# A decoder layer on one core: two pools at the seam of its phases, and GpSimd's mixer work on VectorE

## The chip, the cores and the metric

The kernel runs on one core of a Trainium2 chip. The metric is the time of one execution on the device in microseconds. The kernel before took 2881.92 us in the median of three runs (2880.78 to 2887.45).

## The reference

One post-norm decoder layer in float32 for 2048 tokens of width 1024. The input is modulated and projected by one weight matrix into a gated short convolution (512 channels) and an RWKV-7 time mixing (8 heads of 64); both go through one output projection, a normalisation, a SwiGLU feed-forward part of width 2816 and a second normalisation.

```python
h = x * (1.0 + sc1) + sh1
p = h @ w_in[l]
y_conv = short_conv_mixer(p[..., :N_CONV_COLS], conv_w[l])
y_rwkv = rwkv7_mixer(p[..., N_CONV_COLS:], ...)   # p + mu * (token_shift(p) - p), then a delta-rule scan
mix = jnp.concatenate([y_conv, y_rwkv], axis=-1) @ w_out[l]
x = layer_norm(DEEPNORM_ALPHA * x + (1.0 + gt1) * mix, ln1_g[l], ln1_b[l])
h = x * (1.0 + sc2) + sh2
gate, up = jnp.split(h @ w_ffn_in[l], 2, axis=-1)
f = (jax.nn.silu(gate) * up) @ w_ffn_out[l]
x = layer_norm(DEEPNORM_ALPHA * x + (1.0 + gt2) * f, ln2_g[l], ln2_b[l])
```

## The kernel before, in words

**Products.** Each float32 operand is split into a high half (`act.copy`, a rounding on ScalarE) and a lower half (raw minus high), and a product takes three matmuls (`split`, L230 to L233; `mm3`, L235). The high half is always ScalarE's; the lower half goes to GpSimd (`pool`) unless the caller names VectorE (`dve`).

**Phase 1** (the `with` block at L371) goes over four quarters of 512 tokens. For each quarter `dense` (L259) streams the input weights in half tiles: `half_weight` (L250) loads 256 KB into `raw` (3 buffers), and splits them into `wh` and `wl` (4 buffers each), its lower half on GpSimd. `shifted` (L424) evicts a projected tile with the token shift: ScalarE scales it, VectorE adds the shifted columns, and ScalarE copies the last column into `carry` for the next quarter (L433). Each quarter has four units of two heads (`unit`, L438): preparation (three of its products, `BK` L494, `rk` L497 and `R` L513, are GpSimd's), masked chunk matrices, a triangular solve on VectorE with a small layout through DRAM (`Np` to `Nd` to `Ns`, and back from `Gd` to `H16`, L585 to L609), four further small matmul steps, the chunk scan with one eviction `S` per chunk (L698), and a tail that normalises and stores to `yT` (L734). The solve's first matmul `pz` (L620) reads `LT`, which VectorE transposes from the layout that returns (L613).

**Order of TensorE's work.** TensorE's order is written out by a planner, `Interleave` (L72): the dense stream runs, and units and normalisations are side tasks that yield a cost and a time until their next step. `D_GH` (L51, 15.0) is that time between the issue of the layout that returns and `LT`. The other engines' orders come from the framework's scheduler. All loads and stores are issued by SP, in order.

**The seam.** The output projection of the third quarter runs while the last unit ends. Phase 2 (`with` at L1034) opens the pool `fa` in the memory that phase 1's pool `rw` leaves; a tile of `fa` waits only for the tiles of `rw` whose memory it takes. The tiles named `at...` (L397, L1037) fix the order in memory. `moving(0)` (L1046) makes the first half's moving operands for the feed-forward product: a Strassen-like scheme with seven products (`PRODS`, L976), each with four k of 128. For each k it loads four blocks of h2d (L1057; three into `rawx`, 4 buffers, one into `xr`, 2 buffers), and makes all seven operands of that k: five are a sum on VectorE first (`bh` or `us`, L988), then a high half `uh` on ScalarE and a lower half `ul`, alternately on VectorE and GpSimd. TensorE then takes the products one after the other, each over all four k (L1124 to L1134), 84 matmuls for one block of 128 hidden columns.

**Later.** `weights` (L1091) makes seven weight operands for each block, sums on VectorE, high halves on ScalarE, lower halves `wl` on GpSimd. In the second half of the tokens `scale_weights` (L1165) goes along with the products from the fifth block on: it loads 44 pieces of w_ffn_out, multiplies them on GpSimd with the gate row (L1172), and stores them to `wfs`, for the last product. The last product makes all lower halves (`fl`, `ol`) on VectorE (L1258, L1273).

Of the kernel before, what the change touches and what calls it, by code (L numbers as in the profile page):

```python
# [11 lines left out]
F32 = mybir.dt.float32  # L12
# [7 lines left out]
P = 128  # L20
# [30 lines left out]
D_ST, D_NS, D_TR, D_GH = 1.1, 13.0, 2.0, 15.0  # L51
# [20 lines left out]
class Interleave:  # L72
# [31 lines left out]
    def __call__(self, stream, last=True):  # L104

        more = True
        while more or any(last or not t[3] for t in self.tasks):
            if self.side():
                continue
            cost = next(stream, 0) if more else None  # L110
            if cost == 0:
                more = False
            elif cost is not None:
                self.now += cost
            elif self.tasks and not self.side():
                self.now = min(t for t in [t[0] for t in self.tasks] + self.banks if t > self.now)


@with_exitstack
def kernel(  # L120
# [129 lines left out]
    def half_weight(src, name):  # L250

        raw = f512("raw", "r" + name, 3)
        load(out=raw, in_=src)
        wh = f512("wh", "h" + name, 4, F32R)
        wl = f512("wl", "l" + name, 4, F32R)
        split(wh, wl, raw)
        return wh, wl
# [113 lines left out]
    with ExitStack() as ph1:  # L371
        rw = ph1.enter_context(tc.tile_pool(name="rw", bufs=1))
# [23 lines left out]

        for tag, bufs in (("yc", 1), ("yo", 1), ("sg", 2)):  # L397
            rw.tile([P, QT], F32, tag=tag, name="at" + tag, bufs=bufs)

# [24 lines left out]
        def shifted(q, ps, i, o):  # L424

            a = t2k("A", "A", 1)
            act.activation(a, ps, AF.Identity, scale=omu[:, i:i + 1])
            m = mu[:, i:i + 1]
            dve.scalar_tensor_tensor(out=o[:, 1:QT], in0=ps[:, 0:QT - 1], scalar=m, in1=a[:, 1:QT],
                                     op0=ALU.mult, op1=ALU.add)  # L430
            dve.scalar_tensor_tensor(out=o[:, 0:1], in0=carry[:, q % 2, i:i + 1], scalar=m, in1=a[:, 0:1],
                                     op0=ALU.mult, op1=ALU.add)
            act.copy(out=carry[:, 1 - q % 2, i:i + 1], in_=ps[:, QT - 1:QT])  # L433

        def c3(ap):
            return ap.rearrange("p (c t) -> p c t", t=C)

        def unit(n, q, hp, r, kx, vx, lo):  # L438
# [55 lines left out]
            pool.tensor_tensor(out=BK[:, :, C:2 * C], in0=c3(kP), in1=c3(x2), op=ALU.mult)  # L494

            rk = t2k("sq", "rk" + u)
            pool.tensor_tensor(out=rk, in0=kx, in1=mk, op=ALU.mult)  # L497
# [15 lines left out]
            pool.tensor_tensor(out=R, in0=c3(r), in1=Pc[:, :, 1:C + 1], op=ALU.mult)  # L513
# [520 lines left out]
    with ExitStack() as ph2:  # L1034
        fa = ph2.enter_context(tc.tile_pool(name="fa", bufs=1, reuse_waits="tile"))

        for tag, bufs in (("h26", 8), ("h22", 8), ("h27", 8), ("h24", 8), ("h21", 8), ("h25", 8), ("rawx", 4),  # L1037
                          ("h23", 8), ("us", 1)):
            fa.tile([P, 512], F32, tag=tag, name="at" + tag, bufs=bufs)
# [6 lines left out]
        def moving(half):  # L1046
# [18 lines left out]
            if half == 0:  # L1065
                sums = cycle(lambda: hb[:, 0, :], lambda: hb[:, 1, :], own)
                for k in range(4):
                    raws = {}
                    for b in names:
                        t = (lnp.tile([P, 512], F32, tag="xr", name=f"b{k}_{b}", bufs=2) if b == "21" else  # L1070
                             fa.tile([P, 512], F32, tag="rawx", name=f"b{k}_{b}", bufs=4))
                        raws[b] = fetch(t, b, k)
                    for n, (i, _, terms) in enumerate(PRODS):
                        operand(i, k, terms, raws, n + k)
# [90 lines left out]
        def scale_weights():  # L1165

            for ff in range(FT):
                for m in range(2):
# [3 lines left out]
                    pool.tensor_tensor(out=w, in0=w, in1=rw3[0][:, ms], op=ALU.mult)  # L1172
# [242 lines left out]
```

## Time and profile before

| what | value |
|---|---|
| median of three runs | 2881.92 us (2880.78 to 2887.45) |
| the profiled execution, its own time | 2881.27 us |
| its span, first to last instruction | 2879.5 us |
| TensorE busy (matmuls) | 2660.8 us, 92% |
| VectorE busy | 1898.7 us, 66% |
| ScalarE busy | 1098.7 us, 38% |
| GpSimd busy | 1148.7 us, 40% |
| mean granted clock of TensorE | 0.955 |

In the rows below PE is TensorE's matmuls, PEld its weight loads, DVE VectorE, ACT ScalarE, POOL GpSimd, and SPq the queue of SP, which issues the loads and stores. A name such as `L233` is a line of the kernel, and that line may be a helper's, so the tiles (`uh<-b`: written, then read) say which use it is. A row of waits says who stood still, what released it, for how many microseconds in total, how often, and the longest.

### The profile page before, as it was taken

The numbers are of one execution on the slowest core, as the hardware profiler recorded it, in microseconds if no ns is written. First come the engines' busy times: TensorE is split into PE (matmuls) and PEld (weight loads), VectorE is DVE, ScalarE is ACT, GpSimd is POOL, SyncE is SP. The second block draws the span as 40 slices with busy tenths as digits, with TensorE's granted clock in tenths as the row PEclk, the third lists the DMA queues.
The fourth block names the chain that finished last, engine by engine and source line by source line (L and its number), as shares of the span: only waits on it lengthen the run. The fifth ranks groups of instructions, "written<-read, shape, count | busy, mean of one in ns | idle before, by whom it ended". The sixth has DMA issues, their size and how long they took to land.

```text
span 2879.5 us, 50206 instructions
## 1 busy us (share of the span) xinstructions
PE 2660.8 (92%) x19232; PEld 2082.8 (72%) x19232; DVE 1898.7 (66%) x3133; ACT 1098.7 (38%) x1995; POOL 1148.7 (40%) x935
## 2 busy tenths in 40 slices
PE   7788999999999899998599999997999999998998
PEld 5566677776777677766477788875767887887786
DVE  7354655556445655554573777788988778659697
ACT  4554433334432433434353533333223333332352
POOL 4665333323333333332453544457886442000011
PEclk8888999989999999999799999998999999999999
DMA  6443322233322222224253533233664336655673
GB/s 236 139 129 116 91 62 70 73 104 119 120 69 69 84 66 69 77 72 156 92 179 128 169 105 106 99 99 121 219 213 138 107 102 222 207 179 186 202 237 106
DMA packets 248344, 369.86 MB, mean 128 GB/s; under 512 B 58660, under 2 KB 81188, under 8 KB 248104
## 3 DMA queue, kind: packets, MB, share of 16 engines
q1 hardware_dynamic: 248104, 366.65, 39.5%
q8 instruction: 151, 2.47, 0.3%
q14 instruction: 89, 0.73, 0.1%
HBM read 278.99 MB, written 87.56 MB: 127 GB/s over the span
## 4 chain that ended last, share of the span: by engine, by line
PE 40%; DVE 5%; DMA 4%; POOL 2%; issue 1%; ACT 0%; SPq 0%; POOLq 0%; DVEq 0%; ACTq 0%
PE f L238 8%; PE f L237 8%; PE f L236 8%; PE o L237 4%; PE o L238 4%; PE o L236 4%; PE do L270 3%; DMA wf<-in_wfo_dram 2%; DMA wfs<-wf 2%; POOL wf L1172 1%; DVE c L1007 1%; DVE ws L988 1%; DMA b<-h2d 0%; DVE ul L233 0%; POOL wl L233 0%
## 5 line engine op out<-in xcount | busy, mean ns | idle before, releaser
L236 PE MATMUL f<-uh,wh 128*128 128x512 f32 x1232 | 495.8, 402 | 32.2 <-ACT uh L232 27.7
L238 PE MATMUL f<-uh,wl 128*128 128x512 f32 x1232 | 495.1, 402 | 19.9 <-POOL wl L233 19.7
L237 PE MATMUL f<-ul,wh 128*128 128x512 f32 x1232 | 494.0, 401 | 12.0 <-DVE ul L233 7.2
L233 POOL TENSOR_TENSOR l<-r,h 128x512 fp32r<-128x512 f32 x201 | 265.2, 1321 | 444.8 <-ACT h L232 359.5
L233 POOL TENSOR_TENSOR wl<-ws,wh 128x512 fp32r<-128x512 f32 x220 | 316.3, 1439 | 296.7 <-ACT wh L232 259.5
L236 PEld LDWEIGHTS f<-uh,wh 128*128 128x128 f32 x1232 | 234.8, 191 | 92.8 <-ACT uh L232 31.8
L238 PEld LDWEIGHTS f<-uh,wl 128*128 128x128 f32 x1232 | 234.8, 191 | 85.6 <-POOL wl L233 30.5
L237 PEld LDWEIGHTS f<-ul,wh 128*128 128x128 f32 x1232 | 234.8, 191 | 72.2 <-DVE ul L233 9.4
L232 ACT CAST wh<-ws 128x512 fp32r<-128x512 f32 x220 | 136.7, 621 | 364.7 <-DVE ws L988 259.0
L1007 DVE TENSOR_TENSOR c<-f,c 128x512 f32<-128x512 f32 x264 | 181.2, 687 | 127.6 <-PE f L238 69.7
L988 DVE TENSOR_TENSOR ws<-w,w 128x512 f32<-128x512 f32 x275 | 242.8, 907 | 18.0 <-DMA w<-wfs 7.4
L237 PE MATMUL o<-ol,fh 128*128 128x512 f32 x616 | 243.3, 395 | 8.9 <-DVE ol L233 8.9
L236 PE MATMUL o<-oh,fh 128*128 128x512 f32 x616 | 242.1, 393 | 4.2 <-DVE c L1007 4.1
L238 PE MATMUL o<-oh,fl 128*128 128x512 f32 x616 | 243.7, 396 | 0.0
L232 ACT CAST h<-r 128x512 fp32r<-128x512 f32 x201 | 123.5, 616 | 215.6 <-PE d L270 157.5
L232 ACT CAST fh<-fr 128x512 fp32r<-128x512 f32 x154 | 95.7, 621 | 237.4 <-PE o L237 160.5
L291 POOL TENSOR_SCALAR rsb<-mvb 128x1 f32<-128x1 f32 x16 | 5.7, 356 | 430.2 <-DVE mvb L289 419.6
L233 DVE TENSOR_TENSOR fl<-fr,fh 128x512 fp32r<-128x512 f32 x154 | 106.2, 693 | 94.1 <-ACT fh L232 85.8
L233 POOL TENSOR_TENSOR lo<-ro,ho 128x512 fp32r<-128x512 f32 x64 | 83.6, 1312 | 198.3 <-ACT ho L232 148.4
L233 POOL TENSOR_TENSOR wl<-w,wh 128x512 fp32r<-128x512 f32 x88 | 127.4, 1448 | 49.4 <-ACT wh L232 49.4
L237 PEld LDWEIGHTS o<-ol,fh 128*128 128x128 f32 x616 | 116.7, 189 | 37.1 <-DVE ol L233 10.6
L236 PEld LDWEIGHTS o<-oh,fh 128*128 128x128 f32 x616 | 116.7, 189 | 31.3 <-DVE c L1007 5.7
(498 smaller groups left out, 5800.1 us busy)
## 6 DMA issues: line engine op xcount, KB each, us to landing
r<-in_win_dram SPq DMA_DIRECT2D x201, 256.0 KB
w<-in_wfi_dram SPq DMA_DIRECT2D x176, 256.0 KB
fr<-fd SPq DMA_DIRECT2D x154, 256.0 KB
w<-wfs SPq DMA_DIRECT2D x132, 256.0 KB
fd<-fs SPq DMA_DIRECT2D x110, 256.0 KB
wm<-in_wmod_dram SPq DMA_DIRECT2D x72, 256.0 KB
ro<-in_wout_dram SPq DMA_DIRECT2D x64, 256.0 KB
fd<-th SPq DMA_DIRECT2D x44, 256.0 KB
```

The costliest lines, as they stand in the source:

```text
L232: act.copy(out=hi, in_=raw)
L233: (lo_eng or pool).tensor_sub(lo, raw, hi)
L236: pe.matmul(ps, lh, rh, start=start, stop=False)
L237: pe.matmul(ps, lh, rl, start=False, stop=False)
L238: pe.matmul(ps, ll, rh, start=False, stop=stop)
L270: pe.matmul(ps, l[:, ks], r, start=kk == 0 and i == 0, stop=kk == KT - 1 and i == 2)
L291: pool.tensor_scalar(rs[:, 0:1], mv[:, 1:2], LN_EPS, None, ALU.add)
L988: (eng or dve).tensor_tensor(out=out, in0=blocks[a], in1=blocks[b.lstrip("-")], op=ALU.subtract if b[0] == "-" else ALU.add)
L1007: dve.tensor_tensor(out=c[b, t], in0=in0, in1=in1, op=op)
L1172: pool.tensor_tensor(out=w, in0=w, in1=rw3[0][:, ms], op=ALU.mult)
```

## The change

Seven edits, in the order of the diff: `D_GH` is 18 instead of 15. A class `Pools` sends each tile of a phase to one of two pools by its tag, one from the left and one from the right of the memory; in phase 1 the tags of `EARLY1` go to the left, in phase 2 those of `EARLY2`, so that the tiles of `EARLY2` lie over those of `EARLY1`, and the tiles that fixed the order go. `half_weight` makes its lower half on VectorE. The carry of the token shift is VectorE's. The three products of a unit are VectorE's. `moving(0)` makes the operands of two products for all four k, then of two more, then of three, and loads for each group and k the blocks that it needs, 36 loads instead of 16. `scale_weights` multiplies on VectorE.

```diff
-D_ST, D_NS, D_TR, D_GH = 1.1, 13.0, 2.0, 15.0
+D_ST, D_NS, D_TR, D_GH = 1.1, 13.0, 2.0, 18.0
...
+class Pools:
+    def __init__(self, first, second, early):
+        self.pools, self.early = (second, first), early
+    def tile(self, shape, dtype, name, tag=None, bufs=1):
+        return self.pools[(tag or name) in self.early].tile(shape, dtype, tag=tag or name, name=name, bufs=bufs)
+
+EARLY1 = ("uph", "upl", "blkr", "Ak", "BK", "x2", "tz", "Pi", "ta", "nb", "sq", "cg", "r", "A", "th", "tl", "k", "v", "z", "AK")
+EARLY2 = ("rawx", "h23", "h25", "us")
...
-        split(wh, wl, raw)
+        split(wh, wl, raw, dve)
...
-        rw = ph1.enter_context(tc.tile_pool(name="rw", bufs=1))
+        rw = Pools(ph1.enter_context(tc.tile_pool(name="rw", bufs=1)),
+                   ph1.enter_context(tc.tile_pool(name="rwb", bufs=1, side="right")), EARLY1)
...
-        for tag, bufs in (("yc", 1), ("yo", 1), ("sg", 2)):
-            rw.tile([P, QT], F32, tag=tag, name="at" + tag, bufs=bufs)
...
-            act.copy(out=carry[:, 1 - q % 2, i:i + 1], in_=ps[:, QT - 1:QT])
+            dve.tensor_copy(carry[:, 1 - q % 2, i:i + 1], ps[:, QT - 1:QT])
...
-            pool.tensor_tensor(out=BK[:, :, C:2 * C], in0=c3(kP), in1=c3(x2), op=ALU.mult)
+            dve.tensor_tensor(out=BK[:, :, C:2 * C], in0=c3(kP), in1=c3(x2), op=ALU.mult)
...
-            pool.tensor_tensor(out=rk, in0=kx, in1=mk, op=ALU.mult)
+            dve.tensor_tensor(out=rk, in0=kx, in1=mk, op=ALU.mult)
...
-            pool.tensor_tensor(out=R, in0=c3(r), in1=Pc[:, :, 1:C + 1], op=ALU.mult)
+            dve.tensor_tensor(out=R, in0=c3(r), in1=Pc[:, :, 1:C + 1], op=ALU.mult)
...
-        fa = ph2.enter_context(tc.tile_pool(name="fa", bufs=1, reuse_waits="tile"))
-        for tag, bufs in (("h26", 8), ("h22", 8), ("h27", 8), ("h24", 8), ("h21", 8), ("h25", 8), ("rawx", 4),
-                          ("h23", 8), ("us", 1)):
-            fa.tile([P, 512], F32, tag=tag, name="at" + tag, bufs=bufs)
+        fa = Pools(ph2.enter_context(tc.tile_pool(name="fa", bufs=1, reuse_waits="tile")),
+                   ph2.enter_context(tc.tile_pool(name="fab", bufs=1, reuse_waits="tile", side="right")), EARLY2)
...
-                for k in range(4):
-                    raws = {}
-                    for b in names:
-                        t = (lnp.tile([P, 512], F32, tag="xr", name=f"b{k}_{b}", bufs=2) if b == "21" else
-                             fa.tile([P, 512], F32, tag="rawx", name=f"b{k}_{b}", bufs=4))
-                        raws[b] = fetch(t, b, k)
-                    for n, (i, _, terms) in enumerate(PRODS):
-                        operand(i, k, terms, raws, n + k)
+                for prods in (PRODS[:2], PRODS[2:4], PRODS[4:]):
+                    for k in range(4):
+                        raws = {}
+                        for b in names:
+                            if any(b in (x.lstrip("-") for x in terms) for _, _, terms in prods):
+                                t = (lnp.tile([P, 512], F32, tag="xr", name=f"b{k}_{b}", bufs=2) if b == "21" else
+                                     fa.tile([P, 512], F32, tag="rawx", name=f"b{k}_{b}", bufs=4))
+                                raws[b] = fetch(t, b, k)
+                        for n, (i, _, terms) in enumerate(prods):
+                            operand(i, k, terms, raws, n + k)
...
-                    pool.tensor_tensor(out=w, in0=w, in1=rw3[0][:, ms], op=ALU.mult)
+                    dve.tensor_tensor(out=w, in0=w, in1=rw3[0][:, ms], op=ALU.mult)
```

## Rows read from the trace of the kernel before

**Rows 1.** Stretches: start:end, length, busy of PE, PEld, DVE, ACT, POOL; clock, DMA, GB/s

```profile
130.00:1300.00 1170.00, 1092.92 (x12032) 835.54 (x12030) 641.51 (x1331) 462.43 (x876) 447.38 (x394) 0.96 0.29 88
1300.00:1402.00 102.00, 91.56 (x783) 71.15 (x782) 46.66 (x95) 43.87 (x86) 30.88 (x33) 0.93 0.42 131
1402.00:1452.00 50.00, 15.35 (x34) 9.28 (x35) 38.02 (x44) 19.77 (x33) 27.02 (x19) 0.56 0.33 106
1452.00:1466.00 14.00, 14.00 (x66) 11.38 (x65) 11.00 (x20) 10.98 (x19) 9.46 (x12) 1.00 0.62 225
2000.00:2200.00 200.00, 184.73 (x763) 142.44 (x762) 180.19 (x181) 57.95 (x100) 171.54 (x108) 0.99 0.61 204
2200.00:2400.00 200.00, 200.00 (x859) 161.15 (x858) 153.42 (x200) 65.97 (x113) 96.14 (x73) 1.00 0.30 102
```

**Rows 2.** Waits of PE from 1402 to 1452, grouped by instruction

```profile
L236 PE MATMUL f<-uh,wh 128*128 128x512 f32 x9 | 6.3, 702 | 26.0 <-ACT uh L232 26.0
```

**Rows 3.** Timeline of SP's queue at the seam: start, length, instruction

```profile
1362.16 0.36 SPq L352 DMA_DIRECT2D h2d<-hb  x1
...
1401.75 0.33 SPq L734 DMA_DIRECT2D yT<-yg  x1
1402.12 32.45 SPq L1057 DMA_DIRECT2D b<-h2d  x14
```

**Rows 4.** Groups of VectorE's instructions, 1402 to 1452: count, busy, mean ns, idle before

```profile
L988 DVE TENSOR_TENSOR bh<-b,b 128x512 f32<-128x512 f32 x14 | 13.1, 955 | 8.2 <-DMA b<-h2d 8.2
...
L233 DVE TENSOR_TENSOR ul<-bh,uh 128x512 fp32r<-128x512 f32 x7 | 7.1, 1033 | 0.8 <-ACT uh L232 0.7
```

**Rows 5.** One stretch at the start of the seam, columns as in rows 1

```profile
1402.00:1407.50 5.50, 0.00 (x0) 0.00 (x0) 0.63 (x2) 0.63 (x2) 0.00 (x0) 0.68 0.73 237
```

**Rows 6.** Groups of instructions, 130 to 1300: two of GpSimd, one of VectorE

```profile
L233 POOL TENSOR_TENSOR l<-r,h 128x512 fp32r<-128x512 f32 x186 | 245.9, 1324 | 443.8 <-ACT h L232 358.6 <-PE d L270 34.1 <-PE s L697 17.6
...
L497 POOL TENSOR_TENSOR rk<-k,ta 128x512 f32<-128x512 f32 x15 | 22.3, 1490 | 29.0 <-ACT ta L476 24.7 <-PE ss L484 4.2
...
L572 DVE TENSOR_TENSOR Ym<-sr,kst 128x512 f32<-128x512 f32 x30 | 19.3, 685 | 28.9 <-PE sr L568 28.9
```

**Rows 7.** Who TensorE waited for in the whole span: total us, times, longest us

```profile
PE pz L620 <- DVE LT L613: 18.5, 7, 5.9
...
PE s L697 <- DVE S L698: 8.3, 4, 3.6
PE d L270 <- DVE h_5l L774: 8.0, 2, 5.3
...
PE b L523 <- ACT rkh L232: 5.5, 2, 3.3
```

**Rows 8.** Timeline of ScalarE and VectorE around one carry in the first quarter

```profile
79.31 0.14 ACT L433 COPY carry<-d 128x1 f32<-128x1 f32 x1
...
78.92 0.21 DVE L431 SCALAR_TENSOR_TENSOR k<-carry,vecs,A 128x1 f32<-128x1 f32 x1
```

**Rows 9.** Waits of TensorE from 2000 to 2200

```profile
PE f L238 <- POOL wl L233: 15.1, 17, 1.8
```

**Rows 10.** Groups of instructions of GpSimd and VectorE, 2000 to 2200

```profile
L1172 POOL TENSOR_TENSOR wf<-wf,rws 128x512 f32<-128x512 f32 x43 | 65.3, 1523 | 19.8 <-DMA wf<-in_wfo_dram 12.6 <-issue 5.5 <-POOL wl L233 1.4
...
L988 DVE TENSOR_TENSOR ws<-w,w 128x512 f32<-128x512 f32 x46 | 63.1, 1396 | 4.8 <-DMA w<-in_wfi_dram 4.2 <-issue 0.6
...
L988 DVE TENSOR_TENSOR fs<-th,th 128x512 f32<-128x512 f32 x25 | 32.4, 1342 | 0.7
```

**Rows 11.** The sums of VectorE from 2200 to 2400

```profile
L988 DVE TENSOR_TENSOR ws<-w,w 128x512 f32<-128x512 f32 x53 | 41.0, 808 | 0.0
```

**Rows 12.** Waits of GpSimd from 130 to 1300

```profile
POOL l L233 <- ACT h L232: 358.6, 110, 10.9
```

**Rows 13.** Two waits of the whole span that belong to the last product

```profile
DVE fl L233 <- ACT fh L232: 85.8, 59, 2.3
...
PE o L237 <- DVE ol L233: 8.9, 4, 6.1
```

## The prediction

> **What bounds the kernel now.** I read the stretches first, then who kept TensorE waiting in each, then the queues behind those waits. TensorE is the bound nearly everywhere: in the main part of phase 1 it is busy 1093 of 1170 us, and in a steady stretch of phase 2 it is busy 200 of 200 us with 859 matmuls, 0.233 us each [rows 1]. So a change pays only where TensorE stands still. The reader is to see three such places. The largest is the seam between the phases: in the 50 us from 1402 TensorE is busy 15.4 us, and the granted clock is 0.56, that is, mostly its 1.2 GHz level after standing still, while VectorE is busy 38 us [rows 1]. The second is 2000 to 2200, where TensorE loses 15.3 us with GpSimd busy 171.5 us [rows 1]. The third is spread over phase 1, in single waits of 1 to 6 us.
>
> At the seam the waits are for the first operands of the feed-forward part: 26.0 us for the high half `uh` [rows 2]. What they wait for stood in SP's queue: fourteen loads of h2d issue only from 1402.1, and take 32.5 us to issue, though the last store of the h2d that they read was issued at 1362.2 [rows 3]. Forty microseconds went by with the data there. The code says why: the tiles of `fa` lie in the memory of `rw`, whose last unit stores its output at 1401.8 [rows 3], and the loop makes all seven products' operands of k=0 before it turns to k=1, so that the first product, which needs its four k, waits for 22 of the 28 operands.
>
> **The change part by part.**
>
> *Seam (two pools, three groups of products).* What the first two products need (`rawx`, h23, h25, `us`: 21 tiles) now lies over tiles of `rw` that are dead when the last unit's middle is made, so their eight loads and eight operands can be made between 1362 and 1402, where VectorE is busy under half of the time (46.7 of 102 us from 1300) [rows 1]. They cost VectorE four sums of 0.96 us and four lower halves of at most 1.03 us [rows 4], about 8 us; GpSimd makes the other four. Behind 1402 stand 20 operands. VectorE's work there is its 38.0 us [rows 1] less these 8: 30 us, so 1432 at the earliest. The loads grow from 16 to 36 (2, 3 and 4 for each k, by the code). Eight are early, and six more fit into the free `rawx` and `xr`; 22 remain. After 1402 five moves of 262 KB (the store and four loads) took 5.5 us at 237 GB/s [rows 5], 1.1 us each, so 22 take 24 us, 1426, and the buffers keep the two from overlapping fully. I take 1434 for the last operand, and 1440 for the end of the first block of seven products, since two products (24 matmuls of 0.233 us) stand behind it. Before, 26 of the 84 matmuls were done by 1452 (34, less eight that are transposes by the code), the other 58 take 13.5 us and stand, with eight transposes, in the 14 us to 1466 [rows 1], where the block ends. Gain **26 us**. Bounds: if TensorE never waits, 84 matmuls and two transposes end at 1422, gain 44; if each of the eight later steps of k loads first and then computes, 8 x (3.9 + 3.8) = 61 us to 1463, and 5.6 us more, gain -3. I choose by the VectorE row, because loads of one k and sums of the one before can run together while there are spare buffers.
>
> The Trainium skill, "DMA: Bandwidth & Descriptors", section on bandwidth, speaks against reloading in pieces: it wants transfers of 1 MiB and lists 0.95 us for 64 KB and 6.15 us for 1 MB. Between these a 256 KB load would be some 1.9 us (an estimate from that page), 22 of them 42 us, and the gain 16 us rather than 26. The row of five moves at 1.1 us each decides here, so I keep 26.
>
> *Phase 1, work moved from GpSimd to VectorE.* The lower halves of the streamed weights, 186 in the main part of the phase at 1.32 us on GpSimd [rows 6], 64 more in the output projections, and three mixer products in each of 16 units, such as `rk` at 1.49 us [rows 6]. On VectorE such an operation takes 0.685 us where nothing disturbs it, as the mask of the scan does [rows 6]. That is about 300 x 0.69 = 207 us more on VectorE over some 1500 us, from 55% busy [rows 1] to about 65%, since something comes back: beside GpSimd's work VectorE's own two-operand instructions are stretched, such as a sum to 1.396 us where GpSimd is busiest, against 0.808 in a calmer stretch [rows 10, 11]. None of GpSimd's moved work kept TensorE waiting in phase 1 except through `rk`: the wait for `rkh` is 5.5 us [rows 7]. Taking that product and its queue away gains **4 us** (0 to 5.5). What is late next is VectorE itself: weights have four buffers, about 11 us of cover, so a lower half that comes late is hidden, but the scan's evictions now queue behind lower halves. TensorE's largest waits for VectorE there, other than the layout, are S with 8.3 us and the operands at the start of a quarter, h, with 8.0 [rows 7], and a dozen smaller kinds; I let the busier queue lengthen these two by half: cost **8 us** (bounds: 5 us gained by the shorter instructions, and the second rival).
>
> *Carry on VectorE.* TensorE waits for the carry a few times at the start of the phase, but the carry is only last by a hair: where it ended a wait at 79.45, VectorE's own reading of the same bank had ended at 79.13 [rows 8]. The copy there takes about as long as the 0.21 us of the one-column instruction ahead of it. **0 us** (-2 to 3); ScalarE loses 56 short copies and some idling that nothing waits for.
>
> *Later time for the layout (D_GH 15 to 18).* TensorE waits 18.5 us in seven waits for LT [rows 7]. Three microseconds later, and filled with dense work, takes up to 3 us from each: of the largest, 5.9 us [rows 7], 2.9 stay. At most 15 us; I take **11**, since the last unit has little left to fill with. A unit's chain ends 3 us later, which at the end of the phase can cost 3 us once: lower bound -3.
>
> *Scaling of w_ffn_out on VectorE.* From 2000 to 2200 TensorE waits 15.1 us for GpSimd's `wl` in 17 waits [rows 9]; 43 scalings take 65.3 us of GpSimd there [rows 10]. Without them GpSimd has 106 us of 200, about the 96 of the next stretch [rows 1], where TensorE loses nothing. VectorE, at 180 us of 200, gets 43 x 0.69 to 0.81 = 30 to 35 us, and gets back the stretching: 46 sums at 1.396 against 0.808 us in the next stretch, 27 us, and 25 sums `fs` at 1.34 against 0.69, 16 us [rows 10, 11]. So about 170 of 188 us, tight but under the bound. What it must now wait for are the scaling's loads, 12.6 us of GpSimd's idling now [rows 10], in line ahead of sums and evictions. Gain **11 us** (bounds: 15; and -5, if all of those waits fall on a full VectorE).
>
> **Sum.** 26 + 4 - 8 + 0 + 11 + 11 = 44 us. The profiled execution took 2881.27 us (span 2879.5), 0.65 us under the median of 2881.92, so the sum goes against either: 2838 us.
>
> **The rivals.**
>
> *A. The seam closes by half.* The operands' memory isn't free as early as the code suggests, or SP holds the h2d loads behind weight loads that wait for a buffer, so the first group starts at 1402 after all. Then only the order by groups helps: 36 loads of 1.1 us end at 1442, the last operand stands at about 1448, the block ends at 1454, gain 12 rather than 26: 2852 us. For it: SP's queue is in order, and the loads stood behind the last unit's store at 1401.8. Against it: that store needn't stand ahead of them once the memory is free.
>
> *B. VectorE's queue holds the scan: slower.* In phase 1 GpSimd's lower halves waited 358.6 us for ScalarE's high halves, 110 times, 3.26 us each [rows 12]; on GpSimd this held nobody. On VectorE, in order, whatever stands behind such a wait stands still, S and Np evictions among them. If one in five of the 110 holds an eviction that TensorE needs, 22 x 3.26 = 72 us come in the place of the 8 us counted: 2901 us. It decides from 16 such waits on, one in seven, where the 52 us that the rest gains are used up. Against it: in the last phase VectorE makes the lower halves `fl` in just this way, waits 85.8 us in 59 waits for ScalarE, and TensorE loses 8.9 us to it [rows 13]. The Trainium skill, "TensorE: Matmul & The Clock Gate", in its table at the head, calls VectorE's queue strictly first in, first out, which is what this rival needs; the row on `fl` agrees with it and shows it cheap where no scan stands behind it.
>
> *C. The seam closes wholly*, sums of the second group being made early as well: 44 us there instead of 26, 2820 us. Against it: the tiles of the next products (h21 first) lie over `gu`, which the last unit reads at 1400.
>
> *D. Gains of A with a dearer queue*: seam 12, the queue 28 instead of 8: 2872 us and up, about no change.
>
> **How the numbers follow.** Forecast 0.63, A 0.16, C 0.07, D 0.06, B 0.08. A measurement of this kernel can tell about 0.3%, 9 us, from no change. Faster by more: forecast, A, C and a little of D, 0.87; within it 0.05, slower 0.08. The range takes in C with the layout's and the scaling's upper bounds (2803), and on the other side A and D's near end with the scaling's lower bound (2873).
>
> **What would show it.** In the changed profile: h2d loads issued from about 1365 and again well before the end of the first phase; TensorE busy about half of the 50 us behind the seam, or more, and few waits for `uh` before the first 24 matmuls; waits for LT down to 4 to 7 us; no wait for `wl` near 2000 to 2200 above 4 us, with VectorE under 95%; TensorE's waits for VectorE in phase 1 no more than 10 us above the present. It is wrong if the h2d loads still start behind the last unit's store (A), if waits for S and the h operands grow by tens of microseconds (B), or if the block behind the seam ends within 25 us of its start (C).

## The result, and the profile after

The changed kernel took 2830.48 us in the median of four runs (2828.80 to 2832.34), the kernel before 2881.68 us beside it: a ratio of 0.9818, 95% interval 0.9801 to 0.9835, 51 us faster, where 44 were forecast. The total is near the forecast, and its parts are not. A second measurement on another chip gave 2830.42 us and a ratio of 0.9856 (0.9841 to 0.9870): there the kernel before took 2872.25 us. The gain is 42 to 51 us, and the spread is the kernel before's.

Four points of the program can be found in every trace: the stores to `yT` of the last but one and of the last unit, the first `th` (it comes when five of the seven products of the first block, 60 of its 84 matmuls, are done), and the load of `rws` from `gtd` in the second half. Between them went these microseconds, each the difference of two start times in the profiled execution. The third column is the part of the second in which TensorE stood still:

| kernel | start to last but one unit's store | of it TensorE still | the last unit | its store to the first `th` | to `rws` | to the end | span |
|---|---|---|---|---|---|---|---|
| before | 1345.0 | 114.5 | 56.7 | 61.9 | 525.0 | 890.9 | 2879.5 |
| after | 1299.0 | 87.5 | 73.3 | 49.1 | 519.7 | 887.2 | 2828.3 |
| after, second chip | 1305.6 | 88.7 | 72.6 | 47.0 | 519.4 | 886.1 | 2830.7 |
| seam_alone | 1339.4 | 112.1 | 67.8 | 46.8 | 519.4 | 882.1 | 2855.5 |
| half_alone | 1315.6 | 103.4 | 57.2 | 60.8 | 527.4 | 887.0 | 2848.0 |
| layout_alone | 1331.5 | 104.4 | 56.2 | 60.7 | 525.9 | 890.7 | 2864.9 |
| mixer_alone | 1347.3 | 119.6 | 56.4 | 61.5 | 526.2 | 889.9 | 2881.2 |
| scaling_alone | 1333.7 | 112.4 | 56.4 | 61.6 | 526.3 | 890.4 | 2868.4 |
| weights_apart_2 | 1298.7 | 86.4 | 73.8 | 40.6 | 518.2 | 885.4 | 2816.7 |
| placement_alone | 1341.3 | 115.5 | 55.8 | 61.9 | 515.1 | 877.0 | 2851.0 |
| mixer_back | 1303.7 | 86.2 | 73.5 | 50.2 | 519.6 | 886.7 | 2833.7 |
| carry_back | 1299.2 | 83.2 | 72.6 | 49.0 | 519.6 | 893.7 | 2834.0 |
| apart_placed | 1300.7 | 88.9 | 73.4 | 41.3 | 516.7 | 883.2 | 2815.2 |

In four kernels the work of the first part is that of before (before, seam_alone, which only moves its tiles, scaling_alone, placement_alone), and it took them 1333.7 to 1345.0: a difference under 11 us in that column says little. TensorE's standing still repeats better there, 112.1 to 115.5. Among kernels with the same edit the last unit repeats within 2 us, the next two columns within about 3, the last within 4 to 8.

From before to after the first part gained 46 us, the last unit lost 17, the stretch from its store to the first `th` gained 13, and the rest gained 9. The forecast had 7 for phase 1, 26 for the seam and 11 for the rest.

The same stretches as in [rows 1], in the changed kernel (the second is the 50 us behind the last unit's store, the third lies as far behind the load of `rws` as 2000 to 2200 does before; columns as there):

```profile
130.00:1300.00 1170.00, 1113.26 (x12344) 848.83 (x12342) 743.72 (x1713) 482.45 (x872) 109.02 (x140) 0.97 0.31 94
1372.00:1422.00 50.00, 15.75 (x60) 12.01 (x59) 31.41 (x48) 22.86 (x39) 27.42 (x25) 0.62 0.56 184
1952.60:2152.60 200.00, 183.02 (x755) 141.54 (x755) 163.15 (x223) 55.73 (x99) 94.64 (x65) 0.98 0.61 204
```

In phase 1 TensorE is busy 20 us more, and VectorE only 102 us more, though some 190 us of instructions came to it (below). Behind the seam TensorE still stands still for 34 of 50 us. Over the same work as from 2000 to 2200 before, GpSimd's 171.5 us of [rows 1] are 94.6, and TensorE, busy 183.0 us where it was 184.7, has gained nothing.

Who TensorE waited for, whole span, beside [rows 7, 9]:

```profile
PE f L250 <- ACT wh L246: 45.0, 9, 33.3
PE s L708 <- DVE S L709: 16.3, 7, 8.1
...
PE pz L631 <- DVE LT L624: 9.0, 8, 2.9
...
PE b L534 <- ACT rkh L246: 7.1, 1, 7.1
...
PE d L284 <- DVE h_5l L785: 5.0, 1, 5.0
```

Of the 26 us for `uh` of [rows 2] hardly any are left, and one wait of 33.3 us for a weight's high half `wh` has come. The wait for the scan's `S` doubled, by one of 8.1 us. The layout's wait halved.

SP's queue at the seam shows where the 33 us come from (start, length, instruction, against [rows 3]):

```profile
1311.16 0.33 SPq L1065 DMA_DIRECT2D b<-h2d  x1
...
1321.14 6.69 SPq L1065 DMA_DIRECT2D b<-h2d  x6
...
1347.65 7.95 SPq L1110 DMA_DIRECT2D w<-in_wfi_dram  x3
1372.32 0.33 SPq L745 DMA_DIRECT2D yT<-yg  x1
...
1391.04 10.44 SPq L1065 DMA_DIRECT2D b<-h2d  x6
1401.58 15.59 SPq L1110 DMA_DIRECT2D w<-in_wfi_dram  x8
```

The first group's loads do go out early, from 1311 and in the main from 1321 to 1340, before the last unit's store. But the first block's weights come from four raw blocks, of which two, "22" and "21", use `rawx`, the buffers of the h2d loads. Only three weight loads went out at 1347.7; the next, which the third product needs, stand behind all h2d loads and issue from 1401.6. TensorE took the first 24 matmuls by 1374 and stood until 1407.6. The last of the block's 84 starts at 1425.77, 53.5 us behind the last store; before it started at 1466.30, 64.6 us behind it.

VectorE's timeline in the last unit (start, length, instruction, releaser of the idle time before), and TensorE's matmul that waited for its end:

```profile
1324.66 0.69 DVE L999 TENSOR_TENSOR bh<-b,b 128x512 f32<-128x512 f32 x1 [3.28 <-issue]
...
1330.29 1.77 DVE L999 TENSOR_TENSOR us<-b,b 128x512 f32<-128x512 f32 x1
1332.74 0.69 DVE L247 TENSOR_TENSOR ul<-us,uh 128x512 fp32r<-128x512 f32 x1 [0.68 <-ACT uh L246]
1333.35 0.28 DVE L709 TENSOR_SCALAR S<-s,Pc 128x64 f32<-128x64 f32 x1
```
```profile
1333.68 0.48 PE L708 MATMUL s<-S,MT 64*64 64x64 f32 x4 [8.07 <-DVE S L709]
```

The early operands, with two other instructions among them (`xz`, `lo`), stand in VectorE's queue ahead of one 0.28 us eviction that the scan needs. The Trainium skill, "TensorE: Matmul & The Clock Gate", in its table at the head, has VectorE's queue strictly first in, first out; this row agrees, at 8.07 us. Of the 17 us that the last unit is longer, TensorE stands still for 11 (14.7 where it was 3.6), and its waits for `S` there are 10.4 us, where they were 0.4. In the rest it is busy, and 17 matmuls of the feed-forward part, some 4 us, are among that: they were done ahead and aren't lost.

### The profile page after: what moved, and what is told of

Its sections match the earlier page's. It is cut to its first block, busy times and chain, and to the rows that moved or that the text cites. A ratio compares the mean times of both kernels' runs of the same rounds, so it can differ in the third digit from the quotient of the medians.

```text
span 2828.3 us, 50227 instructions
## 1 busy us (share of the span) xinstructions
PE 2624.5 (93%) x19232; PEld 2065.2 (73%) x19232; DVE 1972.1 (70%) x3543; ACT 1092.6 (39%) x1939; POOL 667.7 (24%) x581
## 4 chain that ended last, share of the span: by engine, by line
PE 40%; DVE 7%; DMA 4%; issue 2%; ACT 0%; POOL 0%; SPq 0%; DVEq 0%; POOLq 0%; ACTq 0%
PE f L252 8%; PE f L251 8%; PE f L250 8%; PE o L251 4%; PE o L250 4%; PE o L252 4%; PE do L284 3%; DMA wf<-in_wfo_dram 1%; DMA wfs<-wf 1%; DVE c L1018 1%; DVE us L999 1%; DMA b<-h2d 1%; DVE wf L1182 1%; DVE ws L999 1%; DVE ul L247 0%
## 5 line engine op out<-in xcount | busy, mean ns | idle before, releaser
L250 PE MATMUL f<-uh,wh 128*128 128x512 f32 x1232 | 489.7, 398 | 46.9 <-ACT wh L246 45.0
L252 PE MATMUL f<-uh,wl 128*128 128x512 f32 x1232 | 489.3, 397 | 15.4 <-POOL wl L247 15.4
L251 PE MATMUL f<-ul,wh 128*128 128x512 f32 x1232 | 487.5, 396 | 8.2 <-DVE ul L247 4.9
L247 POOL TENSOR_TENSOR wl<-ws,wh 128x512 fp32r<-128x512 f32 x220 | 307.2, 1397 | 386.1 <-ACT wh L246 352.9
L247 DVE TENSOR_TENSOR l<-r,h 128x512 fp32r<-128x512 f32 x198 | 145.7, 738 | 142.9 <-ACT h L246 128.6
L999 DVE TENSOR_TENSOR ws<-w,w 128x512 f32<-128x512 f32 x275 | 212.5, 797 | 9.6 <-DMA w<-wfs 6.2
L252 PEld LDWEIGHTS o<-oh,fl 128*128 128x128 f32 x616 | 117.2, 190 | 25.5
L757 POOL COPY zcar<-z 128x2 f32<-128x2 f32 x16 | 6.9, 430 | 454.4 <-DVE z L756 454.4
```

Source lines behind the costliest of these rows:

```text
L247: (lo_eng or pool).tensor_sub(lo, raw, hi)
L250: pe.matmul(ps, lh, rh, start=start, stop=False)
L251: pe.matmul(ps, lh, rl, start=False, stop=False)
L252: pe.matmul(ps, ll, rh, start=False, stop=stop)
L757: pool.tensor_copy(zcar[:, g, :], z[:, QT:QT + 2])
L999: (eng or dve).tensor_tensor(out=out, in0=blocks[a], in1=blocks[b.lstrip("-")], op=ALU.subtract if b[0] == "-" else ALU.add)
```

## The experiments

**seam_alone**: the kernel before with `Pools` and the three groups of products, no other edit.

```diff
-        rw = ph1.enter_context(tc.tile_pool(name="rw", bufs=1))
+        rw = Pools(ph1.enter_context(tc.tile_pool(name="rw", bufs=1)),
...
-                for k in range(4):
+                for prods in (PRODS[:2], PRODS[2:4], PRODS[4:]):
+                    for k in range(4):
```

> The kernel before with the two pools and the groups of products alone, all else as before. The prediction's step gives the seam 26 us: about 2856 us. A second reading, from the profile of the changed kernel: there TensorE does the first two products at once and then waits 33.3 us for the weights of the third, whose raw block shares the four buffers rawx with the h2d loads and so stands behind all of them in SP's queue; the block of seven products then ends 53 us after the output projection instead of 64.5, so the seam gives about 11 us: about 2871 us, with a wait of TensorE for wh of 25 us or more in the seam.

2863.84 us against 2874.17, ratio 0.9962 (0.9948 to 0.9975): 11 us. Its waits at the seam:

```profile
PE f L250 <- ACT wh L246: 26.1, 1, 26.1
PE s L708 <- DVE S L709: 9.4, 3, 8.8
```

The same two waits as after, with GpSimd's work where it was: they belong to the seam's edit. In the table the seam gains 15 us and the last unit loses 11, which leaves 4. The second reading's 11 us came in the total, and its wait for `wh` came too, but most of the gain is where neither reading looked, behind the first `th`: 6 and 9 us in the last two columns before the span. *placement_alone* below is about those.

**weights_apart** and **weights_apart_2**: the changed kernel, with "22" and "21" of the first block in other buffers (`temp`), so that their loads don't wait for `rawx`.

```diff
+                                   temp(f"w{u}_{b}") if half == 0 and ff == FFS[0] else
                                    fa.tile([P, 512], F32, tag="rawx", name=f"w{u}_{b}", bufs=4))
```

> The changed kernel, with the two second-row weight blocks of the first block of hidden columns loaded into the general temporaries instead of rawx, so that they needn't stand behind the h2d loads. If the third product waits for its weights because they share rawx: TensorE's single wait of 33.3 us for wh falls to about 10 us, and what follows waits for the operands of the groups instead; the time falls by about 10 us, to 2820. If the operands of the second group are what is late: no change beyond 3 us.

2821.96 us, ratio 0.9812 (0.9794 to 0.9831) on a chip where the changed kernel wasn't run. So it ran a second time, beside it:

> The changed kernel itself, on the chip of the three runs that follow. Ratio to the kernel before 0.980 to 0.984, as measured. It is here so that the kernel with the weights' buffers apart can be set against it.

> The changed kernel, with the raw weights of the first feed-forward block out of the operands' buffers, a second time, beside the changed kernel. If the 33 us wait for wh was on the path, it ends about 10 us under the changed kernel (the block ended 10 us earlier in its trace): ratio 0.976 to 0.980. If VectorE's and GpSimd's making of the 20 late operands sets the end anyway, it is within 3 us of the changed kernel.

2819.31 us and 0.9821 (0.9805 to 0.9837), against 2830.42 us and 0.9856 for the changed kernel: 11 us. What TensorE waited for behind the last unit is now operands, in short pieces:

```profile
PE f L250 <- ACT uh L246: 7.4, 4, 2.8
PE f L251 <- POOL ul L247: 5.4, 3, 3.3
PE f L251 <- DVE ul L247: 4.5, 2, 3.8
```

The 33 us were on the path. A third of them was the gain, as the operands are the next to be late: TensorE still stands for 17 of the 41 us from the last store to the first `th`.

**half_alone**: the kernel before, lower halves of the phase's weights on VectorE.

```diff
-        split(wh, wl, raw)
+        split(wh, wl, raw, dve)
```

> The kernel before with only the lower halves of half_weight on VectorE. The prediction has this as a cost of 8 us (VectorE's queue): about 2890 us. The second reading: the last unit's middle stores in the changed kernel come up to 46 us earlier, and VectorE's two-operand instructions are no longer stretched by GpSimd's work, so this edit carries most of phase 1's gain: 2850 to 2865 us, with VectorE's rk, BK and Ak near 0.7 us instead of 1.1 to 1.4.

2856.16 us, ratio 0.9937 (0.9920 to 0.9953): 18 us faster. The prediction had it 8 us slower. Groups and stretch from 130 to 1300, against [rows 1, 6, 7]; first groups, then the stretch:

```profile
L233 DVE TENSOR_TENSOR l<-r,h 128x512 fp32r<-128x512 f32 x185 | 136.2, 737 | 137.0 <-ACT h L232 120.7 <-PE d L270 14.4 <-DMA Nd<-Np 1.0
```
```profile
130.00:1300.00 1170.00, 1101.87 (x12200) 840.96 (x12200) 736.99 (x1605) 471.79 (x892) 180.65 (x176) 0.98 0.29 90
```

VectorE waits 121 us for ScalarE's high halves, as the second rival said it would, and TensorE isn't the worse for it: its wait for `S` in this stretch is 8.6 us (before 7.9). Here is TensorE's whole first part, before and in half_alone:

```profile
0.00:1345.04 1345.04, 1230.50 (x12922) 942.71 (x12924) 745.16 (x1555) 546.14 (x1030) 535.46 (x479) 0.94 0.33 100
```
```profile
0.00:1315.64 1315.64, 1212.25 (x12922) 927.70 (x12924) 828.20 (x1793) 546.25 (x1030) 244.66 (x241) 0.96 0.33 102
```

The same 12922 matmuls take TensorE 18 us less, at a granted clock of 0.96 instead of 0.94, and it stands still 11 us less. Over the same two stretches VectorE's products of the triangular solve (`pr`, one in each of its steps, two inputs each), before and in half_alone:

```profile
L603 DVE TENSOR_TENSOR pr<-G,Ns 128x16 f32<-128x16 f32 (+14 forms) x240 | 114.1, 476 | 4.9
```
```profile
L603 DVE TENSOR_TENSOR pr<-G,Ns 128x16 f32<-128x16 f32 (+14 forms) x240 | 76.5, 319 | 3.7
```

VectorE's groups from 130 to 1300, first of the kernel before, then of half_alone, then of the changed kernel (the `rk` shown is the second, of three inputs):

```profile
L498 DVE SCALAR_TENSOR_TENSOR rk<-rk,vecs,r 128x512 f32<-128x512 f32 x15 | 21.3, 1417 | 5.5 <-POOL rk L497 5.5
...
L493 DVE TENSOR_TENSOR BK<-Pi,x 128x512 f32<-128x512 f32 x15 | 19.7, 1312 | 0.1
```
```profile
L498 DVE SCALAR_TENSOR_TENSOR rk<-rk,vecs,r 128x512 f32<-128x512 f32 x15 | 18.5, 1236 | 2.0 <-POOL rk L497 2.0
L493 DVE TENSOR_TENSOR BK<-Pi,x 128x512 f32<-128x512 f32 x15 | 18.4, 1230 | 0.1
```
```profile
L247 DVE TENSOR_TENSOR l<-r,h 128x512 fp32r<-128x512 f32 x185 | 133.5, 722 | 122.7 <-ACT h L246 108.5 <-ACT Gf L664 11.3 <-PE d L284 1.7
...
L509 DVE SCALAR_TENSOR_TENSOR rk<-rk,vecs,r 128x512 f32<-128x512 f32 x15 | 10.8, 718 | 0.0
L504 DVE TENSOR_TENSOR BK<-Pi,x 128x512 f32<-128x512 f32 x15 | 10.2, 681 | 0.0
```

The second reading's time came, and its reason only in part: `rk` and `BK`, which it wanted near 0.7 us, still take 1.24 and 1.23 us in half_alone, where GpSimd makes the mixer products beside them. What the lower halves give back is above all the solve, which that reading didn't name: its 240 products take 38 us less, by far the largest change of any group. They stand on the chain of every unit; how 2.4 us a unit become the 18 us of the kernel is argued, not shown. `rk` and `BK` take half of their time only in the changed kernel, where the mixer products have left GpSimd too (447 us busy before, 181 in half_alone, 109 after). 185 halves at 0.72 us, 40 more in the output projections at 0.69 and 45 mixer products at about 0.72 are some 190 us of new work there, and VectorE's busy time rose by 102. The Trainium skill, "SBUF — State Buffer", section "Who interferes with whom", has a VectorE instruction with two inputs from SBUF contend with a GpSimd instruction that reads SBUF; these rows agree, and give the size: 1312 against 681 ns.

**mixer_alone**: the kernel before, with `BK`'s second half, `rk` and `R` on VectorE (the diff's three lines). **mixer_back**: the changed kernel with the three on GpSimd again.

```diff
-            pool.tensor_tensor(out=rk, in0=kx, in1=mk, op=ALU.mult)
+            dve.tensor_tensor(out=rk, in0=kx, in1=mk, op=ALU.mult)
```

> The kernel before, with the three mixer products alone on VectorE. The prediction: 4 us faster, the wait for rkh (0 to 5.5). What the half-weights' run suggests instead: what leaves GpSimd shortens VectorE's own two-operand instructions beside it, so that the unit's first part (rk, BK, Ak) gets shorter too and the gain is 8 to 14 us (ratio 0.995 to 0.997). Third: VectorE's chain of the unit only gets longer by 3 x 0.7 us, no gain or 3 us slower.

> The changed kernel, with the three mixer products on GpSimd again. Alone they cost the kernel before 8 us. Theory: once the lower halves of the weights have left GpSimd, they cost nothing on VectorE or pay, since no GpSimd work stretches VectorE any more: without them 5 to 15 us slower than the changed kernel (ratio 0.988 to 0.991 where the changed kernel has 0.9856 beside this before). Rival: they cost 8 us in company too, and the changed kernel's first phase is quick through something else (the carry, or layout and weights together): 8 us faster than the changed kernel.

Alone 2881.29 us against 2872.25, ratio 1.0029 (1.0016 to 1.0041): 8 us slower. Its waits from 130 to 1300:

```profile
PE s L697 <- DVE S L698: 11.7, 5, 4.2
PE sk L547 <- DVE Np L537: 11.3, 4, 7.3
PE d L270 <- DVE h_5l L774: 10.9, 2, 6.3
```

These are VectorE's, all three longer than before (7.9, 5.2, 8.0). It is the third reading's direction at more than its price: VectorE's chain of the unit is longer by three instructions that take 0.79 to 1.03 us, and the solve's products, beside GpSimd's lower halves, stay at 452 ns. Taken back out of the changed kernel, the three change nothing that can be told: 2830.78 us, 0.9843 (0.9828 to 0.9858), between the two ratios of the changed kernel. Neither the theory's number nor the rival's came.

**layout_alone**: the kernel before with `D_GH` 18.

```diff
-D_ST, D_NS, D_TR, D_GH = 1.1, 13.0, 2.0, 15.0
+D_ST, D_NS, D_TR, D_GH = 1.1, 13.0, 2.0, 18.0
```

> The kernel before with only D_GH 18 instead of 15. The prediction gives 11 us: about 2871 us, with TensorE's waits for LT at 4 to 7 us instead of 18.5. The rival, that the planner's new order carries most of what phase 1 gained: 2850 us or less. If the order only trades waits for LT against others: 2878 to 2886 us.

2870.85 us against 2874.17, ratio 0.9988 (0.9977 to 0.9999): 3 us. Waits from 130 to 1300, with [rows 7] and these two of before beside them: `pz` 14.8 in 6, `S` 7.9 in 3.

```profile
PE s L697 <- DVE S L698: 12.1, 18, 3.1
PE pd L627 <- ACT Z L622: 7.8, 3, 5.0
PE sk L547 <- ACT AV L543: 7.8, 2, 5.6
...
PE pz L620 <- DVE LT L613: 5.5, 7, 1.8
```

The layout's wait fell by 9 us, to the 4 to 7 that the prediction named, and other waits of the unit (`S`, `Z`, `AV`) rose by 14, while smaller ones fell. It may be that the dense matmuls that fill the three microseconds are missing elsewhere; no run shows it.

**carry_back**: the changed kernel with the carry's copies on ScalarE.

```diff
-            dve.tensor_copy(carry[:, 1 - q % 2, i:i + 1], ps[:, QT - 1:QT])
+            act.copy(out=carry[:, 1 - q % 2, i:i + 1], in_=ps[:, QT - 1:QT])
```

> The changed kernel, with the carry's copies on ScalarE again. The prediction: no difference (-2 to 3 us). Rival: with VectorE fuller and ScalarE the maker of the high halves, the copies in ScalarE's queue hold up more than they did, and the carry on VectorE is worth 5 to 15 us of the first phase.

2834.78 us, 0.9853 (0.9838 to 0.9868), in the middle of what the changed kernel has: no difference, as predicted.

**scaling_alone**: the kernel before with the scaling of w_ffn_out on VectorE.

```diff
-                    pool.tensor_tensor(out=w, in0=w, in1=rw3[0][:, ms], op=ALU.mult)
+                    dve.tensor_tensor(out=w, in0=w, in1=rw3[0][:, ms], op=ALU.mult)
```

> The kernel before, with the scaling of w_ffn_out alone on VectorE. The prediction: 11 us faster (15 to -5), the waits for wl between 2000 and 2200 going from 15 us in 17 to below 4 us. From the stores' times of the changed kernel: 9 us. Rival: VectorE, now over 95% busy there, holds the sums and evictions behind the scaling's loads, and the gain is under 3 us.

2874.62 us against 2872.25, ratio 1.0013 (1.0000 to 1.0026): no gain, if not a loss of 4 us. The rival's number came, though VectorE isn't over 95% busy. Waits of TensorE, and groups, from 2000 to 2200, against [rows 9, 10]:

```profile
PE f L238 <- POOL wl L233: 7.6, 12, 0.9
PE f L236 <- ACT wh L232: 7.4, 5, 2.3
```
```profile
L1172 DVE TENSOR_TENSOR wf<-wf,rws 128x512 f32<-128x512 f32 x40 | 34.8, 871 | 24.0 <-DMA wf<-in_wfo_dram 23.9
L988 DVE TENSOR_TENSOR ws<-w,w 128x512 f32<-128x512 f32 x45 | 34.5, 796 | 0.1
...
L233 POOL TENSOR_TENSOR wl<-ws,wh 128x512 fp32r<-128x512 f32 x46 | 67.5, 1470 | 102.9 <-ACT wh L232 79.2 <-PE f L238 12.9 <-DMA wf<-in_wfo_dram 10.7
```

The sum `ws` did come back from 1.396 to 0.796 us, and VectorE is busy 165 of 200 us. But it now waits 24 us for the scaling's loads, and the rows fit sums that come late behind those waits: GpSimd, free now, stands 79 us waiting for `wh`, and TensorE's 15.1 us are split over `wl` and `wh`. The wait has kept its size and changed its name.

**placement_alone**: the kernel before, with 64 bytes ahead of the operands' pool.

```diff
     with ExitStack() as ph2:
+        ph2.enter_context(tc.tile_pool(name="pad", bufs=1)).tile([P, 16], F32, name="pad")
```

The built program gives each tile its address. In the kernel before, all 56 operands `uh` and `ul` of a half start, in their partition, 1952 bytes past a multiple of 2048. The change put those of five products at 2016 past one, since its second pool hangs from the other end of the memory, and left those of two (`h23`, `h25`) at 1952. Three fences: starts of `th`, one pair a block, of the kernel before and of the changed kernel (two blocks apart), where TensorE never stands still, and starts of matmuls of seam_alone around two changes of pace:

```profile
1661.89 1.15 ACT L1145 ACTIVATE th<-c 128x512 f32<-128x512 f32 x2 [0.29 <-DVE c L1007]
1681.49 1.15 ACT L1145 ACTIVATE th<-c 128x512 f32<-128x512 f32 x2 [0.29 <-DVE c L1007]
```
```profile
1638.89 1.15 ACT L1155 ACTIVATE th<-c 128x512 f32<-128x512 f32 x2 [0.37 <-DVE c L1018]
...
1677.32 1.16 ACT L1155 ACTIVATE th<-c 128x512 f32<-128x512 f32 x2 [0.36 <-DMA w<-in_wfi_dram]
```
```profile
1674.91 0.39 PE L250 MATMUL f<-uh,wh 128*128 128x512 f32 x1
...
1675.59 0.39 PE L250 MATMUL f<-uh,wh 128*128 128x512 f32 x1
...
1681.19 0.39 PE L250 MATMUL f<-uh,wh 128*128 128x512 f32 x1
```

A block took 19.60 us before and 19.22 after (38.43 for two), with the granted clock at 1.00, its 2.4 GHz level, in both. In seam_alone three matmuls take 0.68 us up to 1675.59; the 24 that follow take 5.60 us, 0.233 each as before, and the rest 0.227 again. Twenty-four are what two products have, and counted from the start of the part they are the first two of the seven, whose operands were left at 1952. So:

> The kernel before, with a tile of 64 bytes ahead of the feed-forward operands, so that each of them lies 64 bytes further up in its partition, where the change put five of the seven. Nothing else. Theory: the change moved operands to addresses at which a product's matmuls go by 0.226 instead of 0.233 us, so here a block of 84 takes 19.0 us where TensorE doesn't wait, instead of 19.60, in 44 blocks: 19 to 26 us faster, ratio 0.991 to 0.9935, and all of it behind the seam. Rival: the shorter blocks of the changed kernel come from less of something else beside them (loads, VectorE), and the address does nothing: 19.60 us a block, no change.

2854.32 us against 2875.59, ratio 0.9930 (0.9914 to 0.9947): 21 us from 64 bytes. The stretch from 1620 to 1900, first before, then placement_alone, and its `th`:

```profile
1620.00:1900.00 280.00, 280.00 (x1206) 225.69 (x1205) 214.04 (x279) 95.26 (x167) 134.14 (x101) 1.00 0.33 112
```
```profile
1620.00:1900.00 280.00, 280.00 (x1237) 231.89 (x1236) 206.40 (x290) 95.25 (x165) 138.84 (x103) 1.00 0.35 118
```
```profile
1654.88 1.15 ACT L1146 ACTIVATE th<-c 128x512 f32<-128x512 f32 x2 [0.29 <-DVE c L1007]
1673.92 1.15 ACT L1146 ACTIVATE th<-c 128x512 f32<-128x512 f32 x2 [0.29 <-DVE c L1007]
```

19.04 us a block, 1237 matmuls where there were 1206 in the same 280 us of a TensorE busy throughout, at the same clock. The table has the gain where the theory put it, behind the first `th` (10 and 14 us). In the changed kernel five of seven products have it.

**apart_placed**: the changed kernel with the weights apart, the 64 bytes ahead of `fa` (there they move the other two products), and the scaling on GpSimd again.

```diff
     with ExitStack() as ph2:
+        ph2.enter_context(tc.tile_pool(name="pad", bufs=1)).tile([P, 16], F32, name="pad")
...
+                                   temp(f"w{u}_{b}") if half == 0 and ff == FFS[0] else
                                    fa.tile([P, 512], F32, tag="rawx", name=f"w{u}_{b}", bufs=4))
...
-                    dve.tensor_tensor(out=w, in0=w, in1=rw3[0][:, ms], op=ALU.mult)
+                    pool.tensor_tensor(out=w, in0=w, in1=rw3[0][:, ms], op=ALU.mult)
```

> The changed kernel with the raw weights of the first block apart (11 us faster), with the two products that the change left at the slow addresses moved 64 bytes up (24 of 84 matmuls by 0.007 us in 44 blocks, 7 us), and with the scaling on GpSimd again (from the times between two stores, 0 to 5 us): 2804 to 2815 us, ratio 0.975 to 0.979. If the address does nothing, 2815 to 2820.

2811.07 us, ratio 0.9773 (0.9758 to 0.9789): the best version, some 19 us under the changed kernel's two medians (taken on other chips). That is inside the expected range. The three edits weren't run one by one, but the trace tells two of them: its blocks take 19.04 us (`th` at 1631.89 and 1650.93), 0.18 less than the changed kernel's, in 44 blocks 8 us, and with the 11 us of weights_apart_2 these are the 19. Nothing clear is left for the scaling.

## Why the prediction was right in its total and wrong in its parts

That the total came near is luck. Phase 1 up to the last unit gave 39 us more than its 7, the last unit and the seam together 30 less than their 26, and the rest's 9 are near the 11 forecast for the scaling, which gave nothing.

- **Seam, 26 us: wrong, and by its parts.** The early loads came as forecast, and the last matmul of the block behind the seam still started 54 us after the last store (65 before). The step that failed is the count of what stands behind the moved loads. "The loads grow from 16 to 36" named the h2d loads alone; the weights' "22" and "21" use the same four buffers and stand behind them in SP's queue, so that the third product waited 33.3 us for `wh`. The second failure is "about 8 us" of VectorE's early work taken as free: it stood ahead of the scan's eviction (8.07 us) in a last unit in which TensorE stood 11 us longer. This is near rival B's mechanism, in a place it didn't name. Store to first `th` 13 us gained, last unit 17 lost: the seam's edit by itself gave about nothing in this kernel, 4 us in seam_alone.
- **What the sum lacked.** The address of the operands: 0.38 us a block in 44 blocks, up to 17 us (an estimate), in the two columns behind the first `th`, which show 9 in the changed kernel, 14 in seam_alone and 24 in placement_alone. The prediction took matmuls as 0.233 us each throughout [rows 1].
- **Lower halves on VectorE, cost 8 us: wrong in sign.** The bound was 5 us gained; alone they gain 18. "I let the busier queue lengthen these two by half": `S` and `h` were 7.9 and 8.0 us up to 1300 and are 5.9 and 5.0 after (7.9 and 5.0 on the second chip). The prediction saw the stretched sums, and used them only to size VectorE's load. It had no term for the solve, VectorE's largest group in phase 1, whose products the lower halves on GpSimd had stretched by half.
- **`rk`, 4 us: wrong.** The three products alone cost 8, in company nothing. The wait for `rkh` is 7.1 us (3.7 on the second chip), where it was 5.5.
- **Layout, 11 us: right in direction, the term mis-sized.** 3 alone. The wait fell to 5.5 us alone, as forecast, and to 9.0 in the changed kernel; the step that failed is that the wait's 11 us were taken as the kernel's, since other waits of the unit took its place.
- **Carry, 0: right.**
- **Scaling, 11 us: wrong.** No gain alone. The prediction named the reason among its bounds, 12.6 us of idling for loads "in line ahead of sums and evictions", and chose the other end. After, there are 27.1 us of it over the same work, and TensorE's waits there are 9.6 us for `wl` and 7.2 for `wh`, where they were 15.1.
- **Rivals.** A's 12 us at the seam is nearest in size, by another mechanism. B holds at the seam, not with the 110 waits of phase 1, which on VectorE are 71 of 108.5 us and lengthen no wait of TensorE that can be told. C's condition, a block that ends within 25 us, isn't met even with the weights apart (43 from the last store).
- **The range.** Its lower end is wrongly added: C's 2820 us, with 4 us more each for the layout's and the scaling's upper bounds, is 2812 and not 2803. The result lies inside either.

What stays open is nearly half of the gain. The edits run alone add up to some 20 us (seam 11, halves 18, layout 3, mixer -8, scaling -4), and the changed kernel gains 42 to 51. The mixer's 8 us are gone in company; the other 14 to 23 us come only with the edits together. TensorE's standing still says where some of it is: against the 114 us of the four kernels with the first part of before, half_alone takes off 10 and layout_alone 9, but every kernel that has both takes off 25 to 30, and mixer_back, carry_back, seam_alone and scaling_alone speak against the other edits. A kernel with these two edits alone was not run, and why they gain more together isn't known. In the profiled executions the two have 24 and 8 us of the 39 by which the first part is under the mean of those four (1339.9), but these executions were 6 and 4 us under their kernels' medians. Why 64 bytes matter, and which distance is best, was not tried; nor was a last unit without the early operands on VectorE.

## What to carry to other kernels

When a load is moved ahead, list everything behind it that shares its buffers or its queue, for other operands too, and ask what the next product needs from there. Where VectorE's two-operand instructions take half as long again as they do beside a quiet GpSimd, moving GpSimd's work to VectorE can make VectorE's own chain shorter (the lower halves, 18 us gained) or longer (the mixer products, 8 us lost): run each alone and in company, since edits that gain 18 and 3 alone can gain more together. And when an edit moves tiles in memory, compare the pace of an unbroken run of matmuls before and after: here it was a larger part of the gain than the edit's purpose.

## What the runs showed of the hardware that was not expected

TensorE's pace here depended on where in the partition its moving operand starts: 0.2333 us for a 128x512 matmul of this form at 1952 bytes past a multiple of 2048, 0.2267 at 2016, both at a granted clock of 1.00 and with no wait between. Sixty-four bytes were worth 0.7% of the kernel. The rows show TensorE busy all the time in both, so no view of waits tells of it; only the count of matmuls in a stretch, or the time of a block, does.
